# Latent attention with both parts of the exponentials taken from PSUM, and the softmax sums taken beside the values

## The chip, the core and the metric

The kernel runs on one core of a Trainium2 chip. The metric is the device time of one execution in microseconds (us); lower is better. Five engines work side by side, each through its own instructions in order: PE (TensorE, matrix products into PSUM), DVE (VectorE), ACT (ScalarE), POOL (GpSimd) and SP, which here issues the transfers.

## What is computed

The reference is a backbone of two layers. The change lies in one mixer of the first layer, the latent attention: 8 heads, queries and keys of 96 numbers, values of 64. There are 1024 sample tokens, which read 256 cached context tokens and the 1024 sample tokens, and 256 prompt tokens, which read only themselves.

```python
def mla_keys_values(ckv, kpe, w_kv_b, k_norm):
    kv = (ckv @ w_kv_b).reshape(b, s, H_A, NOPE_DIM + V_DIM)
    k_nope, v = kv[..., :NOPE_DIM], kv[..., NOPE_DIM:]
    ...
def one_block(qblk):
    s = jnp.einsum('bqhd,bkhd->bhqk', qblk, k, preferred_element_type=jnp.float32) * scale
    p = jax.nn.softmax(s, axis=-1).astype(v.dtype)
    return jnp.einsum('bhqk,bkhd->bqhd', p, v)
...
att = block_attention(q, k, v).reshape(b, s, W_A) * jax.nn.silu(g_a)
```

All of it is float32. The kernel gets float32 accuracy from products of a rounded type (fp32r) by splitting each operand into a rounded high part and the small rest, and adding the products high*high, high*low and low*high.

## The kernel before

The attention (`mla`) is written as a list of 176 **steps** (the code calls them slots). A head has three **groups** of queries: G1 (tokens 0 to 511) and G2 (512 to 1023), each against 10 chunks of 128 keys, and G3 (the 256 prompt tokens) against 2 chunks. A step is one chunk of keys for one group, so a head has 10 + 10 + 2 = 22 steps. The order of the instructions on PE, ACT, DVE and POOL is the order in which the program is written (`chained`), and each engine takes its instructions strictly in that order. Within a step the order is set by the table `MORD`; work that belongs to a group but not to a chunk is hung on a step by `at(step, function)`.

What a step does:

- `mla_score`: three products on PE give the transposed scores of one chunk in a PSUM tile `x` (128 keys x 512 queries). Minus the maximum of a query is already in them, as row 96 of the operands.
- ACT takes the exponential of `x` to `p` (SBUF, L1415) and copies it to the rounded part `ph` (L1416).
- `mla_lo`, one step later: DVE subtracts `pl = p - ph` (L1426; POOL for chunk 4), and POOL adds `p` to the running sum `pacc` (L1431).
- `mla_av`, five steps later (`LAG`): two products add `ph` and `pl` against the 128 columns [value high | value low] of the chunk to the PSUM tile `av` (L1439).
- `mla_max` and, a step later, `mla_min`: a tile of 128 queries of a coming group gets its scores in leading parts, in one PSUM tile `S` of three banks (L1364), and DVE takes the maximum over its 1280 columns (L1392). There is one such tile, so the next `mla_max` waits for the `mla_min` before it. `MAHEAD` says how many steps ahead of its group each stands. `mla_shift` then puts the maxima into the queries (four PE transposes, one ACT copy, two steps ahead of the group).

What ends a group: `mla_sums` (the sums of `pacc` over the keys by products with one column of ones), `mla_inv` (DVE's reciprocals of 4 numbers per partition), `mla_row` (four transposes spread them over the rows), `mla_copy` (ACT copies one half of `av`, L1462), `mla_out` (DVE adds the other half, L1467, one step after the copy) and `mla_gate` (ACT copies the inverses; for odd heads POOL multiplies with the gate and the values, L1478 and L1482). `MEND` holds the steps on which these stand.

The PSUM banks of this stage: 3 for `S`, 2 for `x`, 1 for the transposes `pt`, 2 for `av`. The values come from `prep_k`, which writes them split to DRAM (`d_V`), and `load_head` reads a head's back. Behind the last step, `out0_steps` (the output projection) fills waiting PE with products listed in `FILL`; its last row of operands needs the gated result of the last two heads (`out0_mix(3, ...)`).

Of the kernel before, what the change touches and what calls it, by code (L numbers as in the profile page):

```python
# [18 lines left out]
P = 128  # L19
# [6 lines left out]
EPS = 1e-6  # L26
# [12 lines left out]
ACCV = 7  # L39
FILL = (0, 0, 1, 0, 0, 0, 1, 1, 1, 1, 1, 1, 1, 0, 0, 0, 0)  # L40
# [10 lines left out]
PLO = (4,)  # L51
PB = LAG + 2
MORD = ('load_head', 'out0_mix_load', 'out0_mix', 'out0_w', 'mla_av', 'mla_inv', 'mla_min', 'mla_lo', 'mla_max', 'mla_copy', 'mla_out', 'mla_shift', 'mla_gate', 'mla_row', 'load_k', 'mla_sums')
# [13 lines left out]
class Rows:  # L67
    """Exact float32r parts of [1024, tokens], a tile for each group of tokens: [:, k, tokens of one group]."""
# [17 lines left out]
class Kern:  # L86
# [17 lines left out]
    def chained(self, *engines):  # L104
        """What is traced inside issues in the order of the trace on each of engines."""
# [18 lines left out]
    def rsqrt_steps(self, pool, out, ss, n, width):  # L124
        """out = (ss / n + EPS) ** -0.5, by the integer seed and three Newton steps."""
# [16 lines left out]
    def split_w(self, src, n, short=False, tag="w"):  # L142
        """DRAM [128, n] -> exact float32r parts in SBUF; short: in less time, with a half on DVE."""
# [60 lines left out]
    def main(self, ctx):  # L204
# [5 lines left out]
        # scratch in DRAM  # L210
# [69 lines left out]
    def mod_rows(self, ps, rows, tag, bufs=None):  # L280
        """2 * silu of both conditions, on every partition; yields before each of the four copies."""
# [138 lines left out]
    def start_square(self, scr, o, y, eng):  # L420
        """Sums over half y of d, but for the partitions, of the squares of 256 tokens."""
# [5 lines left out]
    def start_sum(self, scr, sums, y):  # L427
        """Sums over the partitions; of two tiles of tokens at columns 2 * y + tile."""
# [12 lines left out]
    def start_h(self, t, hh, hl, r, o, n, k):  # L441
        """Block k of h of tokens o..o+n; r: rows of rstd."""
# [63 lines left out]
    def mod_gate(self, lp, pr):  # L506
        """Two blocks of the gate of layer 1, with the same rows; the last of them ends it."""
# [26 lines left out]
    def small_start(self, sp, wp):  # L534
# [3 lines left out]
        # gains of the transposed rows  # L538
# [45 lines left out]
    def small_out(self, sp):  # L584
# [45 lines left out]
        # rotary key, gain in; the sum of squares of the raw key tail  # L630
# [13 lines left out]
        # rotary tables with the query gain in  # L644
# [60 lines left out]
    def mlstm_stab(self):  # L705
        """The stabilisers from chunk to chunk, and the weights of the states with them; yields between its small steps."""
# [19 lines left out]
    def gate_silu2(self, out, ps):  # L726
        """out = 2 * silu(ps)"""
# [4 lines left out]
    def gate_unit(self, pool, hh, hl, u, dst, groups=GROUPS, bufs=2):  # L732
        """2 * silu of a block of columns, to DRAM; yields between its groups of tokens."""
# [40 lines left out]
    def stream(self, units, hh, hl):  # L774
        """Projections by blocks of 128 columns; yields between their products. The last unit's weights are only made ready."""
# [17 lines left out]
    def drive(self, main, side):  # L793
        """The products of main, and between them the steps of side, which yields how many columns may pass before its next."""
# [6 lines left out]
    def mlstm(self, mp, hh, hl, hs):  # L801
        """The heads' projections, and between their products the steps of the heads' other work."""
# [109 lines left out]
        # decay matrices  # L912
# [32 lines left out]
        # states at the start of each chunk  # L945
# [26 lines left out]
        # outputs  # L972
# [164 lines left out]
    def prep_k(self, pp, s, x):  # L1137
# [12 lines left out]
        V = pp.tile([P, 4, P], F32R, name="V", tag="V", bufs=3)  # L1150
        pv = ps.rearrange("p (s h e) -> p s h e", s=2, h=4)
        nc.scalar.activation(tok[:, :, 0:64], pv[:, 0], AF.Copy)
        sq = pp.tile([P, 4, 64], F32, name="sqa", tag="sqa", bufs=2)
        nc.scalar.activation(sq, pv[:, 0], AF.Square)
        nc.scalar.activation(V[:, :, 0:64], pv[:, 1], AF.Copy)
        nc.vector.tensor_tensor(V[:, :, 64:P], pv[:, 1], f(V[:, :, 0:64]), op=ALU.subtract)
        nc.sync.dma_start(self.d_V[4 * hf:4 * hf + 4, :, i, :].rearrange("h p e -> p h e"), f(V))
# [57 lines left out]
    def prep_head(self, pool, s, h):  # L1215
        """Scaled transpose of a head's [tok, 96] tiles as float32r parts, to DRAM."""
# [20 lines left out]
    def mla(self):  # L1237
        """Transposed scores of a head's group of queries against a chunk of 128 keys per step; the maximum of a query
        is taken ahead, over the scores of the leading parts, and enters the product as a row of its operands."""
# [4 lines left out]
        with ExitStack() as es:  # L1244
            self.ps_x = es.enter_context(self.pool(name="psAx", bufs=2, space=PSUM))
            self.ps_t = es.enter_context(self.pool(name="psAt", bufs=1, space=PSUM))
            self.ps_s = es.enter_context(self.pool(name="psAs", bufs=2, space=PSUM))
# [3 lines left out]
            groups, slots, jobs, todo = [], [], {}, {}  # L1251

            def at(s, fn, *a):
                todo.setdefault(s, []).append((fn, a))
            for h in range(8):
                for o, n in GROUPS:
# [11 lines left out]
                    e, w = len(slots) - 1 + LAG, MEND[n]  # L1268
                    at(e + w[0], self.mla_copy, heads, G)
# [1067 lines left out]
```

## Time and profile before

| what | value |
|---|---|
| three timed runs | 1816.31, 1817.76 (median), 1823.14 us |
| profiled execution, span from first to last instruction | 1810.9 us |
| median minus this span | 6.9 us |
| busy shares over the span | PE 94%, DVE 70%, ACT 48%, POOL 46% |
| attention, from the first score product to the last | 625.4 to 953.1 us, 327.7 us, 41.0 us a head |

The profile has no time of its own for the profiled execution beside its span; the 6.9 us are what lies around it and what runs differ by. The busy shares are means over stages with different limits, so the stage of the attention has to be read by itself: which engine is busy there, and which wait ends last.

### The profile page before, as it was taken

How to read it: one execution, taken by the hardware profiler on the slowest of the kernel's cores; microseconds unless marked ns; L12 is line 12 of the kernel's file. 1: busy time of each engine (PE TensorE's matmuls, PEld its weight loads, DVE VectorE, ACT ScalarE, POOL GpSimd, SP SyncE). 2: the span in 40 equal slices, each digit the busy share in tenths (PEclk: the TensorE clock that was granted, in tenths of full speed). 3: DMA queues.
4: the chain of work that ended last, by engine and by line, in shares of the span. 5: the costliest groups of instructions: out<-in, count | busy, mean ns of one | idle time of the engine just before them, and what ended most of it. 6: DMA issues, size and time to landing. Idle time of an engine off the chain costs nothing.

```text
span 1810.9 us, 27853 instructions
## 1 busy us (share of the span) xinstructions
PE 1701.9 (94%) x9238; PEld 1468.2 (81%) x9238; DVE 1259.9 (70%) x3221; ACT 870.1 (48%) x1976; POOL 840.5 (46%) x783
## 2 busy tenths in 40 slices
PE   7799899999999989998899999999999999899999
PEld 7688788887878777776778879999888888788877
DVE  6878985788884899999994386556551221788852
ACT  4455665454534477777773343322111111678740
POOL 3534551113131288878884552335232321577741
PEclk9899999999999999989899999999999999999999
DMA  7326675233421372323205442447681112888836
GB/s 250 107 77 184 203 216 187 58 117 56 114 73 31 106 193 78 89 78 89 75 24 175 158 159 94 163 160 272 215 217 67 64 45 81 244 233 231 241 126 192
DMA packets 145601, 250.97 MB, mean 139 GB/s; under 512 B 21554, under 2 KB 77106, under 8 KB 145458
## 3 DMA queue, kind: packets, MB, share of 16 engines
q1 hardware_dynamic: 145314, 248.54, 45.9%
q8 instruction: 73, 1.20, 0.3%
q14 instruction: 70, 0.57, 0.1%
q0 software_dynamic: 144, 0.66, 0.1%
HBM read 167.71 MB, written 81.43 MB: 138 GB/s over the span
## 4 chain that ended last, share of the span: by engine, by line
PE 61%; DVE 23%; DMA 5%; issue 5%; ACT 3%; SPq 1%; POOL 1%; DVEq 0%; ACTq 0%; POOLq 0%
PE mm L842 9%; PE mm L170 5%; PE mm L169 5%; PE mm L168 5%; DVE pl L1426 4%; PE mm L1752 3%; PE mm L1750 3%; PE mm L1751 3%; DVE st L1392 2%; PE mm L785 2%; PE av L2184 2%; PE av L1439 2%; PE mm L1913 1%; PE mm L1592 1%; PE mm L1593 1%
## 5 line engine op out<-in xcount | busy, mean ns | idle before, releaser
L151 POOL TENSOR_TENSOR wl<-ws,wh 128x1024 fp32r<-128x1024 f32 (+1 forms) x60 | 148.6, 2478 | 354.9 <-ACT wh L149 323.3
L1426 DVE TENSOR_TENSOR pl<-p,ph 128x512 fp32r<-128x512 f32 (+1 forms) x161 | 208.3, 1326 | 4.9 <-ACT ph L1416 4.5
L1431 POOL TENSOR_TENSOR pacc<-pacc,p 128x512 f32<-128x512 f32 x125 | 188.9, 1511 | 19.3 <-ACT p L1415 12.6
L170 PE MATMUL mm<-h1h,wl 128*128 128x512 f32 (+1 forms) x480 | 171.6, 357 | 0.0
L168 PE MATMUL mm<-h1h,wh 128*128 128x512 f32 (+1 forms) x480 | 171.5, 357 | 0.0
L169 PE MATMUL mm<-h1l,wh 128*128 128x512 f32 (+1 forms) x480 | 171.5, 357 | 0.0
L842 PE MATMUL mm<-hl,wh 128*128 128x512 f32 (+1 forms) x432 | 164.7, 381 | 0.0
L842 PE MATMUL mm<-hh,wh 128*128 128x512 f32 (+1 forms) x432 | 162.9, 377 | 0.0
L842 PE MATMUL mm<-hh,wl 128*128 128x512 f32 (+1 forms) x432 | 161.6, 374 | 0.0
L1415 ACT ACTIVATE p<-x 128x512 f32<-128x512 f32 (+1 forms) x176 | 101.1, 575 | 78.9 <-PE x L1411 53.6
L149 ACT ACTIVATE wh<-ws 128x1024 fp32r<-128x1024 f32 x60 | 63.4, 1057 | 115.4 <-PE mm L169 61.6
L1416 ACT ACTIVATE ph<-p 128x512 fp32r<-128x512 f32 (+1 forms) x176 | 107.8, 612 | 5.6
L1750 PE MATMUL mm<-awh,h1h 128*128 128x384 f32 x320 | 108.6, 339 | 0.0
L1752 PE MATMUL mm<-awh,h1l 128*128 128x384 f32 x320 | 107.5, 336 | 0.0
L1751 PE MATMUL mm<-awl,h1h 128*128 128x384 f32 x320 | 107.4, 336 | 0.0
L169 PEld LDWEIGHTS mm<-h1l,wh 128*128 128x128 f32 x480 | 90.2, 188 | 14.7
L170 PEld LDWEIGHTS mm<-h1h,wl 128*128 128x128 f32 x480 | 90.3, 188 | 14.4
L168 PEld LDWEIGHTS mm<-h1h,wh 128*128 128x128 f32 x480 | 90.2, 188 | 14.5
L1392 DVE TENSOR_REDUCE st<-S 128x1 f32<-128x1280 f32 (+1 forms) x68 | 94.0, 1382 | 5.5 <-PE S L1364 5.3
L842 PEld LDWEIGHTS mm<-hh,wl 128*128 128x128 f32 x432 | 82.7, 191 | 8.5
L842 PEld LDWEIGHTS mm<-hh,wh 128*128 128x128 f32 x432 | 82.7, 192 | 8.5
L842 PEld LDWEIGHTS mm<-hl,wh 128*128 128x128 f32 x432 | 82.7, 192 | 7.9
(474 smaller groups left out, 5075.1 us busy)
## 6 DMA issues: line engine op xcount, KB each, us to landing
adar<-adaR SPq DMA_DIRECT2D x64, 256.0 KB, 2.8
ws<-evB SPq DMA_DIRECT2D x24, 512.0 KB, 3.7
ws<-odB SPq DMA_DIRECT2D x20, 512.0 KB, 3.4
d_V<-V SPq DMA_DIRECT2D x32, 256.0 KB, 2.5
ws<-wout SPq DMA_DIRECT2D x16, 512.0 KB, 3.4
k<-d_k SPq DMA_DIRECT2D x7, 1152.0 KB, 11.0
q<-d_q SPq DMA_DIRECT2D x7, 960.0 KB, 6.7
Vh<-d_V SPq DMA_DIRECT2D x8, 768.0 KB, 5.0
```

The source lines that it names most:

```text
L151: nc.gpsimd.tensor_tensor(lo[:, :m], st[:, :m], f(hi[:, :m]), op=ALU.subtract)
L168: nc.tensor.matmul(ps[:, :n], a, hh[:, k, o:o + n], start=(k == 0), stop=False)
L169: nc.tensor.matmul(ps[:, :n], a, hl[:, k, o:o + n], start=False, stop=False)
L170: nc.tensor.matmul(ps[:, :n], b, hh[:, k, o:o + n], start=False, stop=(k == KB - 1))
L842: nc.tensor.matmul(ps[:, :n], (wh, wh, wl)[z % 3][:, k * P:(k + 1) * P], (hh, hl, hh)[z % 3][:, k, o:o + n], start=(z == 0), stop=(z == 3 ...
L1392: self.nc.vector.tensor_reduce(out, src, axis=AX.X, op=ALU.max, negate=True)
L1416: nc.scalar.activation(hi[:, :n], p[:, :n], AF.Copy)
L1426: eng.tensor_tensor(lo[:, :n], p[:, :n], f(hi[:, :n]), op=ALU.subtract)
L1431: eng.tensor_tensor(G["acc"][:, :n], (G["acc"] if kc > 1 else G["p"][0][0])[:, :n], p[:, :n], op=ALU.add)
L1750: nc.tensor.matmul(ps[:, :N], a, wh[:, k, :], start=(k == 0), stop=False)
L1751: nc.tensor.matmul(ps[:, :N], a, wl[:, k, :], start=False, stop=False)
L1752: nc.tensor.matmul(ps[:, :N], b, wh[:, k, :], start=False, stop=(k == KB - 1))
```

## The change

Six parts, all in the attention and in the layout of its values:

1. ACT takes the exponential twice from the PSUM tile `x`: once to the rounded `ph` in SBUF, once back into `x` itself. `p` is gone. DVE's `pl` is `x - ph`, with `x` in PSUM. `x` therefore stays in use until `mla_lo` has read it. There are three `x` tiles now, and `mla_shift` takes its transposes from the same three.
2. `pacc` on POOL adds up `ph`. The values carry a block of 64 columns of ones ([low | high | ones] for even heads, [ones | high | low] for odd). `ph` is multiplied with [low | high] into `av0`, `pl` with [high | ones] into `av1`, so the sums of `pl` grow beside the values in `av1`.
3. `mla_sums` is one plain float32 product of a block [zeros | ones] with `pacc` over all the queries, into `av1`. The four small products, the small reciprocals and the four transposes are gone.
4. Chunk 9 (the last chunk of G1 and G2) has no parts: one exponential, no subtraction, no place in `pacc`, and one plain float32 product of [high | ones] with `p` into `av1`; its values are kept whole in the place of the high part.
5. `mla_out`: ACT copies halves of `av0` and `av1`, DVE adds twice, all on one step. For odd heads `mla_gate` has DVE take a reciprocal of 128x512 (128x256 for G3). `av0` and `av1` have one tile each, so a group's first value product waits for the `mla_out` before it; the value products start three steps (`AVGAP`) behind the end of the group before, and go two chunks a step until they have caught up.
6. `MORD` puts `mla_sums` and `mla_out` ahead of `mla_lo`, and `mla_lo` ahead of `mla_min`; POOL no longer takes any subtraction; `load_V` reads values into two lasting tiles, in pieces of 512 bytes.

```diff
-MEND = {512: (1, 2, 0, 1, 1, 2, 3), 256: (1, 2, 0, 4, 1, 2, 5)}
+NAT = 9
-PB = LAG + 2
-MORD = ('load_head', ..., 'mla_av', 'mla_inv', 'mla_min', 'mla_lo', 'mla_max', 'mla_copy', 'mla_out', 'mla_shift', 'mla_gate', 'mla_row', 'load_k', 'mla_sums')
+AVGAP = 3
+PB = LAG + 4
+MORD = ('load_head', ..., 'mla_av', 'mla_sums', 'mla_out', 'mla_lo', 'mla_min', 'mla_max', 'mla_shift', 'mla_gate', 'load_k', 'load_V')
 ...
-            self.ps_x = es.enter_context(self.pool(name="psAx", bufs=2, space=PSUM))
-            self.ps_t = es.enter_context(self.pool(name="psAt", bufs=1, space=PSUM))
-            self.ps_s = es.enter_context(self.pool(name="psAs", bufs=2, space=PSUM))
+            self.ps_x = es.enter_context(self.pool(name="psAx", bufs=3, space=PSUM))
+            self.ps_v = es.enter_context(self.pool(name="psAv", bufs=1, space=PSUM))
 ...
+                    e = end + AVGAP
+                    for c in range(G["nk"]):
+                        e = max(e, G["first"] + c + LAG)
+                        avs.setdefault(e, []).append((G, c))
+                        if len(avs[e]) == 2:
+                            e += 1
+                    end = max(x for x in avs)
+                    at(end, self.mla_sums, G)
+                    at(end + 1, self.mla_out, heads, G)
+                    at(end + 2, self.mla_gate, heads, G)
 ...
     def mla_score(self, hp, heads, G, kc):
-        nc.scalar.activation(p[:, :n], S[:, :n], AF.Exp)
-        nc.scalar.activation(hi[:, :n], p[:, :n], AF.Copy)
+        if kc == NAT:
+            nc.scalar.activation(p[:, :n], S[:, :n], AF.Exp)
+            return
+        nc.scalar.activation(hi[:, :n], S[:, :n], AF.Exp)
+        nc.scalar.activation(S[:, :n], S[:, :n], AF.Exp)
     def mla_lo(self, hp, G, kc):
-        eng = nc.gpsimd if kc in PLO and not end else nc.vector
-        eng.tensor_tensor(lo[:, :n], p[:, :n], f(hi[:, :n]), op=ALU.subtract)
+        nc.vector.tensor_tensor(lo[:, :n], S[:, :n], f(hi[:, :n]), op=ALU.subtract)
 ...
+        if kc == NAT:
+            nc.tensor.matmul(av[1][:, :n], f(one), p[0][:, :n], start=False, stop=False)
+            return
+        nc.tensor.matmul(av[0][:, :n], both, p[0][:, :n], start=(kc == 0), stop=last)
+        nc.tensor.matmul(av[1][:, :n], one, p[1][:, :n], start=(kc == 0), stop=False)
+    def mla_sums(self, G):
+        self.nc.tensor.matmul(G["av"][1][:, :n], self.zo[:, c:c + P], G["acc"][:, :n], start=False, stop=True)
+    def mla_out(self, heads, G):
+        nc.scalar.activation(v, a[other, :n], AF.Copy)
+        nc.scalar.activation(r, b[other, :n], AF.Copy)
+        nc.vector.tensor_tensor(v, a[mine, :n], v, op=ALU.add)
+        nc.vector.tensor_tensor(v, b[mine, :n], v, op=ALU.add)
     def mla_gate(self, heads, G):
+        nc.vector.reciprocal(r, r)
```

How the instructions stand now, at the end of G2 of head 0. On DVE, `pl` rows are `mla_lo`, `st` rows with 1280 columns read are `mla_min`, `pv` rows are `mla_out`. Before:

```order
L1392 TENSOR_REDUCE st<-S 128x1
L1426 TENSOR_TENSOR pl<-p,ph 128x512
L1451 RECIPROCAL st<-pt 128x4
L1426 TENSOR_TENSOR pl<-p,ph 128x512
L1467 TENSOR_TENSOR pv_7400<-av,pv_7400 64x512
```

The same place on DVE in the changed kernel:

```order
L1452 TENSOR_TENSOR pl<-x,ph 128x512
L1488 TENSOR_TENSOR pv_7400<-av_7675,pv_7400 64x512
L1489 TENSOR_TENSOR pv_7400<-av_7676,pv_7400 64x512
L1452 TENSOR_TENSOR pl<-x,ph 128x512
L1414 TENSOR_REDUCE st<-S 128x1
L1452 TENSOR_TENSOR pl<-x,ph 128x512 x2
```

There are two additions now, and they stand ahead of the step's `mla_lo` and `mla_min`; before, the one addition stood behind `mla_lo`, a step after the copy that it needs.

ACT at the same place, changed kernel, where `pv` and `pr` are the two copies that the additions and the gate need:

```order
L1441 ACTIVATE ph<-x 128x512
L1442 ACTIVATE x<-x 128x512
L1486 ACTIVATE pv_7400<-av_7675 64x512
L1487 ACTIVATE pr_7403<-av_7676 64x512
```

Both copies stand behind both exponentials of their own step; before, one copy stood there, and the copy to `pr` three exponentials later.

PE at the same place, changed kernel: the end of G2 (chunk 9, then the sums), a maximum, the scores of the next two steps, and the next maximum:

```order
L1467 MATMUL av_7676<-p,Vh_7339 128x512
L1476 MATMUL av_7676<-pacc,zo 128x512
L1386 MATMUL S<-k_7337,q 128x512 x2
L1386 MATMUL S<-k_7337,q 128x256
L1431 MATMUL x<-q,k_7337 128x512
L1432 MATMUL x<-q,k_7337 128x512
L1433 MATMUL x<-q,k_7337 128x512
```

Behind these come the three score products of one more step and then the next three `S` products, with no value products between. In the kernel before, PE stands thus there, with value products in every step:

```order
L1439 MATMUL av<-pl,Vh 128x512
L1364 MATMUL S<-k_7337,q 128x512 x2
L1364 MATMUL S<-k_7337,q 128x256
L1409 MATMUL x<-q,k_7337 128x512
L1410 MATMUL x<-q,k_7337 128x512
L1411 MATMUL x<-q,k_7337 128x512
L1439 MATMUL av<-ph,Vh 128x256
L1439 MATMUL av<-pl,Vh 128x256
```

So the two steps behind a group's end have moved from five products each to the three score products, and the steps after them carry seven.

More of the change, by code (lines that the diff above doesn't have):

```diff
@@ L50 @@
 LAG = 5
-PLO = (4,)
-PB = LAG + 2
-MORD = ('load_head', 'out0_mix_load', 'out0_mix', 'out0_w', 'mla_av', 'mla_inv', 'mla_min', 'mla_lo', 'mla_max', 'mla_copy', 'mla_out', 'mla_shift', 'mla_gate', 'mla_row', 'load_k', 'mla_sums')
+AVGAP = 3
+PB = LAG + 4
+MORD = ('load_head', 'out0_mix_load', 'out0_mix', 'out0_w', 'mla_av', 'mla_sums', 'mla_out', 'mla_lo', 'mla_min', 'mla_max', 'mla_shift', 'mla_gate', 'load_k', 'load_V')
 DB = 128
@@ L1250, in mla @@
             self.load_pair(hp, heads, 0)
-            groups, slots, jobs, todo = [], [], {}, {}
+            self.zo = hp.tile([P, 192], F32, name="zo")
+            nc.gpsimd.memset(self.zo, 1.0)
+            nc.gpsimd.memset(self.zo[:, 64:P], 0.0)
+            groups, slots, avs, todo = [], [], {}, {}
             def at(s, fn, *a):
                 todo.setdefault(s, []).append((fn, a))
+            end = -AVGAP
             for h in range(8):
@@ L1285, in mla @@
             with self.chained(E.PE, E.Activation, E.DVE, E.Pool):
-                groups[0]["st"] = hp.tile([P, 8], F32, name="st", tag="st", bufs=5)
-                for s in range(min(todo), max(max(todo), len(slots) + LAG) + 1):
+                for s in range(min(todo), max(todo) + 1):
                     if 0 <= s < len(slots):
@@ L1292, in mla @@
                             self.mla_lo(hp, *slots[s - 1])
-                        if m == "mla_av" and 0 <= s - LAG < len(slots):
-                            self.mla_av(heads, *slots[s - LAG])
+                        if m == "mla_av":
+                            for x in avs.get(s, []):
+                                self.mla_av(heads, *x)
                         for fn, a in todo.get(s, []):
@@ L1301, in mla @@
                         fill = self.out0_steps(A, 0, self.pre, 0, KB - 1)
-                    if s >= len(slots) + FILL[0]:
-                        for _ in range(FILL[1 + s - len(slots) - FILL[0]]):
-                            next(fill, None)
+                    if s >= len(slots) and FILL[s - len(slots):][:1] == (1,):
+                        next(fill, None)
+                for _ in fill:
+                    pass
             self.out0_mix(3, 0, 512, src=heads[7][4][:, 0:512])
@@ L1327, in load_head @@
             self.kts += [self.mlap.tile([P, 2, 1536], F32R, name=f"k{x}") for x in range(3)]
+            self.vts = [self.mlap.tile([P, 12, 192], F32R, name=f"Vh{x}") for x in range(2)]
+            for x, c in enumerate((P, 0)):
+                nc.gpsimd.memset(f(self.vts[x][:, :, c:c + 64]), 1.0)
         k = self.kts[h % 3]
-        V = self.mlap.tile([P, 12, P], F32R, name="Vh", tag="Vh", bufs=2)
+        V = self.vts[h % 2]
         if h > 0:
@@ L1422, in mla_lo @@
         n = G["n"]
-        p, hi, lo = G["p"][kc]
-        end = (G["h"], G["o"]) >= (7, 512)
-        eng = nc.gpsimd if kc in PLO and not end else nc.vector
-        eng.tensor_tensor(lo[:, :n], p[:, :n], f(hi[:, :n]), op=ALU.subtract)
+        if kc == NAT:
+            return
+        hi, lo, S = G["p"][kc]
+        nc.vector.tensor_tensor(lo[:, :n], S[:, :n], f(hi[:, :n]), op=ALU.subtract)
         if kc == 1:
-            G["acc"] = hp.tile([P, 512], F32, name="pacc", tag="pacc", bufs=3)
+            G["acc"] = hp.tile([P, 512], F32, name="pacc", tag="pacc", bufs=2)
@@ L1429, in mla_lo @@
         if kc > 0:
-            eng = nc.vector if end and (kc >= ACCV or G["o"] == TS) else nc.gpsimd
-            eng.tensor_tensor(G["acc"][:, :n], (G["acc"] if kc > 1 else G["p"][0][0])[:, :n], p[:, :n], op=ALU.add)
+            nc.gpsimd.tensor_tensor(G["acc"][:, :n], G["acc"][:, :n] if kc > 1 else f(G["p"][0][0][:, :n]), f(hi[:, :n]), op=ALU.add)
     def mla_av(self, heads, G, kc):
         nc = self.nc
-        n, V = G["n"], heads[G["h"]][2]
+        n, V, y = G["n"], heads[G["h"]][2], G["h"] % 2
@@ L1436, in mla_av @@
         if kc == 0:
-            G["av"] = self.ps_s.tile([P, 512], F32, name="av", tag="av")
-        for x in (1, 2):
-            nc.tensor.matmul(G["av"][:, :n], V[:, G["kb"] + kc, :], G["p"][kc][x][:, :n], start=(kc == 0 and x == 1),
-                             stop=(kc == G["nk"] - 1 and x == 2))
-    def mla_sums(self, hp, G):
-        nc = self.nc
-        nt = G["n"] // P
-        G["r"] = pt = self.ps_t.tile([P, 512], F32, name="pt", tag="t") if nt == 4 else G["av"][:, 256:512]
-        for x in range(nt):
-            nc.tensor.matmul(pt[:, x:x + 1], G["acc"][:, x * P:(x + 1) * P], self.ones[:, 0:1], start=True, stop=True)
@@ L1449, in mla_inv @@
-    def mla_inv(self, G):
-        nt = G["n"] // P
-        self.nc.vector.reciprocal(G["st"][:, 4:4 + nt], G["r"][:, 0:nt])
-    def mla_row(self, G):
-        for x in range(G["n"] // P):
-            self.nc.tensor.transpose(G["r"][:, x * P:(x + 1) * P], G["st"][:, 4 + x:5 + x].to_broadcast([P, P]), self.ident)
-    def mla_copy(self, heads, G):
+            G["av"] = [self.ps_v.tile([P, 512], F32, name=f"av{x}", tag=f"av{x}") for x in range(2)]
+        av, p, c = G["av"], G["p"][kc], G["kb"] + kc
@@ new lines, in mla_av @@
+        both, one = V[:, c, 64 * y:64 * y + P], V[:, c, 64 - 64 * y:192 - 64 * y]
+        if kc == NAT:
+            nc.tensor.matmul(av[1][:, :n], f(one), p[0][:, :n], start=False, stop=False)
+            return
+        last = kc == (G["nk"] if G["nk"] <= NAT else NAT) - 1
+        nc.tensor.matmul(av[0][:, :n], both, p[0][:, :n], start=(kc == 0), stop=last)
+        nc.tensor.matmul(av[1][:, :n], one, p[1][:, :n], start=(kc == 0), stop=False)
+    def mla_sums(self, G):
+        n, c = G["n"], 64 - 64 * (G["h"] % 2)
+        self.nc.tensor.matmul(G["av"][1][:, :n], self.zo[:, c:c + P], G["acc"][:, :n], start=False, stop=True)
```

58 lines of the change are left out of this document (29 added, 29 removed).

## The prediction

> **What bounds the kernel now.** I read the busy time of the attention's stage first, then its groups by shape, then its waits, then the instructions one by one. The header of the first row is PE, PEld (weight loads), DVE, ACT, POOL, granted PE clock, DMA share, GB/s.
>
> ```profile
> span 1810.9 us, 27853 instructions
> 625.90:958.00 332.10, 296.80 (x1373) 235.40 (x1371) 320.22 (x284) 243.69 (x429) 272.91 (x186) 0.94 0.33 91
> L1409 PE MATMUL x<-q,k x176: 283/399/775, 625.4 to 953.1; 97*128 97x512 f32 x160, 97*128 97x256 f32 x16
> ...
> L1426 DVE TENSOR_TENSOR pl<-p,ph 128x512 fp32r<-128x512 f32 x145 | 193.7, 1363 | 4.8 <-ACT ph L1416 4.5
> L1416 ACT ACTIVATE ph<-p 128x512 fp32r<-128x512 f32 x160 | 101.1, 632 | 5.1
> L1415 ACT ACTIVATE p<-x 128x512 f32<-128x512 f32 x160 | 95.1, 595 | 78.7 <-PE x L1411 53.6 <-issue 14.8 <-POOL pacc L1431 6.6
> L1467 DVE TENSOR_TENSOR pv<-av,pv 64x512 f32<-64x512 f32 x16 | 10.9, 684 | 0.2
> L1462 ACT ACTIVATE pv<-av 64x512 f32<-64x512 f32 x16 | 9.5, 591 | 3.1 <-PE av L1439 2.8
> L1517 ACT ACTIVATE mxh<-mxl,sc 128x512 fp32r<-128x512 f32 x7 | 4.9, 707 | 0.0
> ...
> PEld S L1364 <- DVE st L1392: 30.0, 19, 3.1
> PE S L1364 <- DVE st L1392: 22.1, 17, 2.7
> ```
>
> DVE is busy 320.2 of 332.1 us: it is the bound. Its subtractions take 193.7 of that. PE (296.8, and its records overlap) waits for DVE's maxima. The 176 scores run from 625.4 to 953.1: 327.7 us, 41.0 a head of 22 steps.
>
> The subtraction is slow for a reason that single rows show:
>
> ```profile
> 947.23 1.77 DVE L1426 TENSOR_TENSOR pl<-p,ph 128x512 fp32r<-128x512 f32 x1
> 715.54 0.65 DVE L1426 TENSOR_TENSOR pl<-p,ph 128x512 fp32r<-128x512 f32 x1
> 652.86 1.41 DVE st L1392
> 706.23 0.40 PE L1411 MATMUL x<-q,k 96*128 96x512 f32 x1
> 706.46 0.40 PE L1439 MATMUL av<-ph,Vh 128*128 128x512 f32 x1
> ...
> 706.94 0.75 PE L1364 MATMUL S<-k,q 96*128 96x512 f32 x3
> 707.53 0.40 PE L1409 MATMUL x<-q,k 97*128 97x512 f32 x1
> ...
> 519.79 0.38 PE L1040 MATMUL cps<-kT,qT 128*128 128x128 f32 x2
> 520.01 0.60 PE L1041 MATMUL cps<-Cst,qT 128*128 128x258 f32 x2
> ```
>
> The same subtraction takes 0.65 or 1.77 us; the addition with one operand in PSUM (L1467) averages 0.684, like the short one. PE starts a 512-column product every 0.23 us (706.23 to 706.46) and needs 0.59 for the three of a maximum (706.94 to 707.53). A plain float32 product comes as two records: 0.22 us for 128 columns (519.79 to 520.01), so four times that, 0.87, for 512.
>
> **The change, part by part.** *Subtraction.* 18 a head at 0.68 (L1467's row) in place of 1.363; ends 0.65 and 1.36 (if POOL still holds it up). I take 0.68, since one operand is in PSUM as in that row. DVE's work per head is then 18 x 0.68 + 8 maxima x 1.41 + 4 additions x 0.68 + about 3 for the small shapes and the mix = 29.3 us without reciprocals, where 320.2 / 8 = 40.0 stood. *ACT.* The copy of 0.632 becomes an exponential that ends in PSUM. No row writes there from ACT; the nearest is 0.595 (L1415), which I take. Below, 0.5 would change each gap under 0.1 us; above, if reading and writing one bank excluded each other, 1.19. *Chunk 9.* PE 0.87 for two products (0.46), minus one subtraction. *Sums.* 0.87 for eight small records and four transposes of about 1.2: even. So PE's work per head is 20 x 3 + 18 x 2 products x 0.233 + 8 x 0.59 + 5 plain ones, 4 of 0.87 and one of half, + 3.4 for G3's shapes and the shifts = about 33.4 us. *Values.* The parts in `prep_k` have as many elements as before. Loads of 512-byte pieces are wanted some 16 steps after they are issued, and the longest load of before took 14.0 us; `load_V` waits on SP for a head's last products, and behind it queue loads of the coming head. Nothing, with 30 us of cover. The memsets on POOL lie ahead of the first step.
>
> So by work alone PE would be the bound and 8 x (41.0 - 33.4) would be won. But PE, ACT and DVE take their instructions in order, and an `x` tile is now free only after `mla_lo`. I followed the order through one head with these durations; PE stands still in three places (steps counted from a head's first chunk).
>
> *End of G2 (step 2).* From the end of the sums product: maximum 0.59, score 0.70 and 0.16 to its last column, two exponentials 1.19, copy `pv` 0.59, two additions 1.37, `mla_lo` 0.68, `mla_min` 1.41, and about 0.15 of handing over: 6.85 us, and only then may the next `mla_max`, on step 4, write `S`. PE has the maximum and two scores meanwhile, 2.0 us. It idles 4.9. The additions are the turn: they wait for ACT's copies, which stand behind the exponentials of their own step, and `mla_lo` and `mla_min` wait behind them on DVE, ready long since.
> *End of G3 (step 5).* The same on step 6 with half-size pieces: score 8 needs the tile of score 5, whose `mla_lo` stands behind the additions. PE idles 2.1, and 0.4 for the maximum that the shift needs.
> *End of G1 (step 14).* From the last column of score 15: exponentials 1.24, mix copy 0.71, DVE's part of the mix and the additions 0.8 + 1.37, `mla_lo` 0.68 = 4.8; only then score 17. PE has 1.15 of it: idle 3.65.
> With 0.4 at the last shift, a head takes 33.4 + 4.9 + 2.5 + 3.65 + 0.4 = 44.8 us.
>
> *Reciprocals.* Three for each odd head, of 512, 512 and 256 per partition. The only rows are small:
>
> ```profile
> L1451 DVE RECIPROCAL st<-pt x16: 167/169/183, 656.0 to 959.5; 128x4 f32<-128x4 f32 x16
> L1451 DVE RECIPROCAL st<-av x8: 155/157/171, 682.8 to 962.9; 128x2 f32<-128x2 f32 x8
> ```
>
> Two more elements cost 12 ns, 6 ns each: 512 take 0.15 + 3.07 = 3.2 us, 256 take 1.7. The cheap end is an ordinary DVE operation, 0.68. I take 3.2, the only reciprocal rows there are. They hold up `mla_lo` and `mla_min` behind them. Followed through: G2's and G3's, on steps 4 and 7 of the next head, cost 2.9 together (their rest falls into time in which PE waits anyway), G1's on step 16 costs 2.8: 5.7 a pair of heads. At 0.68 it would be 1.1.
> The Trainium skill, "VectorE: DVE Perf Modes", section "First, the fixed hardware budget", says that the reciprocal runs an iterative divide with a repeat count of 8. If that is eight cycles an element, 512 take an estimated 4.4 us; a pair would pay 8.7 and the sum below would end at 1892.
>
> *The clock.* After idle time PE runs at half rate here (the seventh column is the granted clock; starts 0.43 apart, not 0.23):
>
> ```profile
> 653.00:656.00 3.00, 1.68 (x12) 1.60 (x13) 2.78 (x3) 1.07 (x2) 2.92 (x3) 0.98 0.22 85
> 656.00:659.00 3.00, 3.00 (x8) 2.35 (x9) 2.96 (x5) 1.23 (x2) 2.86 (x3) 0.50 0.00 0
> 657.19 0.63 PE L1439 MATMUL av<-ph,Vh 128*128 128x512 f32 x1
> 657.62 0.63 PE L1439 MATMUL av<-pl,Vh 128*128 128x512 f32 x1
> 773.00:776.00 3.00, 1.30 (x7) 0.72 (x5) 3.00 (x3) 2.91 (x6) 2.91 (x3) 1.00 0.00 0
> 776.00:779.00 3.00, 3.00 (x18) 2.65 (x19) 3.00 (x2) 0.87 (x2) 2.50 (x2) 1.00 0.00 0
> ```
>
> It happened after 1.3 us of idling at 654 and not after 1.7 at 774. Half rate for 3 us costs PE 1.6. If it follows both long gaps of every head, a pair pays 3.3 (part falls into the waiting); I count half, 1.6.
> The Trainium skill, "TensorE: Matmul & The Clock Gate", section "HAM oscillation — how this bites in real kernels", has the clock halved once idle time crosses a window of about 3.4 us. Both gaps are longer; by that rule the sum ends 7 us later, at 1886.
>
> *The end.* The last row of the output projection needs the last gate:
>
> ```profile
> 956.51 0.40 PE L1591 MATMUL S<-mxh,wh 128*128 128x512 f32 x1
> ...
> 965.72 0.39 PE L1593 MATMUL S<-mxh,wl 128*128 128x512 f32 x1
> 963.82 0.72 ACT L1517 ACTIVATE mxh<-mixa,sc 128x512 fp32r<-128x512 f32 x1 [2.77 <-POOL mixa L1482]
> ```
>
> From the last sums of G2 it is copies 1.2, additions 1.4, reciprocal 3.2, POOL's two products 2.6, split 1.5 = 9.9 us; PE has about 5.5 (seven rows of 0.70 as filling, G3's products). That is 4 us more than now, where PE hardly waits.
>
> **The sum.** A pair: 2 x 44.8 + 5.7 + 1.6 = 96.9. Four pairs 387.6, minus 2.9 that the first head doesn't inherit: 384.7. Against 327.7: +57.0, and 4 at the end: +61. The span goes from 1810.9 to 1872; with the 6.9 by which the median lies above that span, 1879 us.
>
> **The rivals.**
> 1. *The relief wins (faster).* If the engines run far enough ahead that the additions hold up nobody, odd heads are bound by DVE (29.3 + 2 x 3.2 + 1.7 = 37.4) and even ones by PE (33.4): 4 x 70.8 = 283, -41 with the end: 1777. For it speaks that DVE is the bound now by 320 of 332. Against it: the chain at step 2 is all in the written order, and one `S` tile cannot be run ahead of. It decides where PE idles under 7.6 us a head; I count 11.4.
> 2. *Cheap reciprocals.* At 0.68: 4 x (89.6 + 1.1 + 1.6) = 369, +41 and 2 at the end, 1861. Still slower; this is inside the first case.
> 3. *Slow exponential into PSUM.* At 1.19 ACT has some 41 us a head and each chain grows by 0.6: 2 to 4 more a head, 1895 to 1911. A subtraction that POOL still holds up (1.36) adds 18 x 0.68 = 12 to DVE, which at 41.5 and reciprocals goes the same way or beyond: the change would then not do what it says.
> 4. *They balance*, with gaps of 7 to 8 us a head: within 9 us of before.
>
> **How the numbers follow.** 0.66 for the forecast with its own range of 1845 to 1895 (cheap reciprocals and no halved clock at one end, slow ones and both halvings at the other); 0.14 for the third; 0.14 for the first; 0.06 for the balance. A measurement here tells changes of about 0.5% (9 us) from none: faster 0.14, same 0.06, slower 0.80. The range of 1835 to 1925 takes in the forecast and most of the third case and leaves out the first and the balance.
>
> **What would show it.** In the changed profile `pl` should take about 0.68, DVE should fall clearly below nine tenths in the stage, and the longest waits should be PE's `S` products for `st` and PE's scores for `pl`, with `pv` additions ahead of both waiting for ACT; the reciprocals should show 3 to 4 us. I am wrong if PE is busy without gaps through steps 2 to 4 and 15 to 17, if the scores span under 330 us, or if the stage is as slow as I say but for another engine.

## The result, and the profile after

The changed kernel takes 1882.6 us (median of four runs, 1879.0 to 1885.9); the kernel before, run beside it, took 1817.0. The ratio is 1.036, with a 95% interval of 1.033 to 1.039: slower by some 65 us. The forecast was 1879. The profiled execution has a span of 1880.5 us, 69.6 more than before. Each profile shows one execution, and executions of one kernel lie up to 12 us apart (the kernel before: 1811.3 to 1823.1 us), so a few us between two profiles need not come from an edit.

The first fence is the page's span line, then the row of the stage (its window, its length, then busy time of PE, PEld, DVE, ACT and POOL, granted clock, DMA share, GB/s), then the row of the 176 scores with their first and last start:

```profile
span 1880.5 us, 27299 instructions
628.00:1024.00 396.00, 319.13 (x1191) 240.29 (x1192) 247.95 (x291) 214.87 (x412) 198.00 (x162) 0.86 0.29 77
L1431 PE MATMUL x<-q,k x176: 282/396/988, 628.4 to 1022.1; 97*128 97x512 f32 x160, 97*128 97x256 f32 x16
```

DVE, which was busy 96% of this stage, is busy 63% now, so the relief that the change aims at is real. But the scores span 393.7 us where they spanned 327.7, no engine is busy all the time, and the granted clock is 0.86 where it was 0.94. The 69.6 us come apart from these rows alone: the scores start 3.0 us later (628.4 against 625.4), span 66.0 more, and what follows the last score takes 0.6 more (858.4 against 857.8).

The groups of the same stage (busy, mean ns of one, idle before them and for whom), then, from the view of the waits, PE's and DVE's longest (us in total, times, longest):

```profile
L1452 DVE TENSOR_TENSOR pl<-x,ph 128x512 fp32r<-128x512 f32 x144 | 95.0, 679 | 59.8 <-ACT x L1442 59.4
L1414 DVE TENSOR_REDUCE st<-S 128x1 f32<-128x1280 f32 x60 | 88.7, 1479 | 1.3 <-PE S L1386 1.3
L1441 ACT ACTIVATE ph<-x 128x512 fp32r<-128x512 f32 x144 | 86.0, 597 | 145.8 <-PE x L1433 142.9
L1442 ACT ACTIVATE x<-x 128x512 f32<-128x512 f32 x144 | 85.4, 593 | 0.0
L1499 DVE RECIPROCAL pr<-pr 128x512 f32<-128x512 f32 x7 | 23.4, 3342 | 0.0
L1499 DVE RECIPROCAL pr<-pr 128x256 f32<-128x256 f32 x3 | 5.2, 1741 | 0.0
...
PE x L1431 <- DVE pl L1452: 38.9, 15, 4.3
PE S L1386 <- DVE st L1414: 34.6, 8, 4.8
DVE pv L1488 <- ACT pv L1486: 31.4, 10, 4.4
```

Each operation has the price that was taken for it: the subtraction 0.679 us (0.68), the exponential into PSUM 0.593 (0.595), the reciprocals 3.34 and 1.74 (3.2 and 1.7). And the engines wait in a circle: PE for DVE's subtractions and maxima, DVE for ACT's copies, ACT (142.9 us) for PE's scores.

The circle is seen one instruction at a time at the end of G2 of head 1. The timeline gives start, duration, instruction, and in brackets the idle time of its engine before it and who ended it:

```profile
724.66 0.40 PE L1433 MATMUL x<-q,k 96*128 96x512 f32 x1
724.94 0.59 ACT L1442 ACTIVATE x<-x 128x512 f32<-128x512 f32 x1
725.55 0.59 ACT L1486 ACTIVATE pv<-av 64x512 f32<-64x512 f32 x1
726.17 0.69 DVE L1488 TENSOR_TENSOR pv<-av,pv 64x512 f32<-64x512 f32 x1 [3.81 <-ACT pv L1486]
727.00 0.69 DVE L1489 TENSOR_TENSOR pv<-av,pv 64x512 f32<-64x512 f32 x1
727.71 0.69 DVE L1452 TENSOR_TENSOR pl<-x,ph 128x512 fp32r<-128x512 f32 x1
728.31 1.48 DVE L1414 TENSOR_REDUCE st<-S 128x1 f32<-128x1280 f32 x1
729.85 1.44 PE L1386 MATMUL S<-k,q 96*128 96x512 f32 x3 [4.79 <-DVE st L1414]
730.31 3.34 DVE L1499 RECIPROCAL pr<-pr 128x512 f32<-128x512 f32 x1
731.51 0.63 PE L1432 MATMUL x<-q,k 96*128 96x512 f32 x1
```

DVE does nothing for 3.81 us and waits at the head of its queue for the copy. Behind that come `pl`, whose exponential (L1442) ended at 725.53, and the maximum, whose products ended at 723.65, one after the other, and only then may PE write `S` again: 4.79 us of idling, where 4.9 had been worked out. Behind the stop PE's products take 0.63 us, not 0.40, and start 0.43 apart, not 0.23: half rate.

### The profile page after: what moved, and what is told of

Same layout as the page of the kernel before. It is cut to its first block, busy times and chain, and to the rows that moved or that the text cites. A ratio compares the mean times of both kernels' runs of the same rounds, so it can differ in the third digit from the quotient of the medians.

```text
span 1880.5 us, 27299 instructions
## 1 busy us (share of the span) xinstructions
PE 1726.0 (92%) x9046; PEld 1473.0 (78%) x9046; DVE 1193.4 (63%) x3228; ACT 842.3 (45%) x1960; POOL 766.1 (41%) x760
## 4 chain that ended last, share of the span: by engine, by line
PE 67%; DVE 19%; DMA 4%; ACT 4%; issue 3%; POOL 1%; SPq 1%; DVEq 0%; ACTq 0%; POOLq 0%
PE mm L841 9%; PE mm L169 5%; PE mm L168 5%; PE mm L167 5%; PE mm L1773 2%; PE mm L1774 2%; PE mm L1772 2%; PE mm L784 2%; PE x L1431 2%; PE av L1471 2%; PE av L1470 2%; PE x L1433 2%; PE x L1432 2%; PE av L2206 2%; PE S L1386 2%
## 5 line engine op out<-in xcount | busy, mean ns | idle before, releaser
L1456 POOL TENSOR_TENSOR pacc<-pacc,ph 128x512 f32<-128x512 f32 x112 | 143.3, 1280 | 63.8 <-ACT ph L1441 59.4
L1441 ACT ACTIVATE ph<-x 128x512 fp32r<-128x512 f32 (+1 forms) x160 | 92.2, 576 | 148.5 <-PE x L1433 145.4
L1452 DVE TENSOR_TENSOR pl<-x,ph 128x512 fp32r<-128x512 f32 (+1 forms) x160 | 101.8, 653 | 72.1 <-ACT x L1442 71.5
L1431 PE MATMUL x<-q,k 97*128 97x512 f32 (+1 forms) x176 | 85.9, 488 | 42.2 <-DVE pl L1452 38.9
L1442 ACT ACTIVATE x<-x 128x512 f32<-128x512 f32 (+1 forms) x160 | 91.4, 571 | 0.0
```

The costliest lines, as they stand in the source:

```text
L1431: nc.tensor.matmul(S[:, :n], k[0:97, 0, c], q[0:97, 0, qs], start=True, stop=False)
L1452: nc.vector.tensor_tensor(lo[:, :n], S[:, :n], f(hi[:, :n]), op=ALU.subtract)
L1456: nc.gpsimd.tensor_tensor(G["acc"][:, :n], G["acc"][:, :n] if kc > 1 else f(G["p"][0][0][:, :n]), f(hi[:, :n]), op=ALU.add)
```

## The experiments

Each kernel was timed beside the kernel before. Differences between kernels are differences of their medians; the ratio to the kernel before has its interval. Three of the first four put right one suspect each in the changed kernel, and one (e3) moves half of the suspected order.

**The written order (e1).** The table of the order within a step:

```diff
-'mla_av', 'mla_sums', 'mla_out', 'mla_lo', 'mla_min', 'mla_max', 'mla_shift', 'mla_gate',
+'mla_av', 'mla_sums', 'mla_lo', 'mla_min', 'mla_max', 'mla_out', 'mla_shift', 'mla_gate',
```

> One edit: on a step, the subtractions, the maximum of a tile and the next tile's products stand ahead of the group's copies and additions (the table of the order within a step). Theory of the written order: the long stops come from additions that wait for late copies while ready DVE work stands behind them. Then the subtraction and the maximum behind a group's end come some 2 to 3 us sooner, a head costs about 40 us instead of 44.7, and the time falls by 25 to 60 us, most likely 45, to about 1837. The waits of the S products for st and of the scores for pl shrink to less than half. Rival 1, the reciprocals alone make the stops: they stay where they are, so under 10 us of change. Rival 2, the ring of three x tiles is too short as such, whatever the order: under 10 us of change.

Measured: 1832.3 us, ratio 1.009 (1.007 to 1.012), 50 less than the change. No work is added or taken away, and on DVE the edit only puts a subtraction and a maximum ahead of two additions, so three quarters of the loss were their order. Both rivals fall. The waits for `pl` and for `S` fell from 38.9 and 34.6 us to about half, a little short of the "less than half" that was expected. Stops were only one part of what came back: PE's idle time in the stage falls from 77 us to 50, but its busy time falls as much, from 319 us to 292, and the granted clock is 0.94 again, as in the kernel before (PE's waits in the stage, then e1's stage):

```profile
PE x L1431 <- DVE pl L1452: 20.3, 11, 2.6
PE S L1386 <- DVE st L1414: 18.9, 16, 4.2
...
628.00:970.00 342.00, 291.95 (x1174) 213.50 (x1173) 246.76 (x287) 212.13 (x408) 193.08 (x158) 0.94 0.33 88
```

**The reciprocals (e2).** The kernel leaves out the division by the softmax sums.

```diff
-        nc.vector.reciprocal(r, r)
+        nc.vector.tensor_scalar(r, r, 1.0, None, op0=ALU.mult)
```

> One edit: the reciprocal of each odd head's gate becomes an ordinary DVE operation of the same shape (a multiplication by one), so the division by the softmax sums is left out. Prediction's price: 5.7 us a pair of heads at 3.2 us a piece and 1.1 at 0.68, so four pairs should fall by about 18 us, and the end by 2: about 1862. Rival 1, the reciprocals are the main cost: 40 us or more, to 1840 or below. Rival 2, they lie beside PE's idle time: under 6 us.

Measured: 1867.3 us, ratio 1.029 (1.026 to 1.032), 15 less than the change where 18 in the stage and 2 at the end had been priced. The scores span 381.8 us here, 12 less. The reciprocals are a smaller part, as forecast; the main loss stays without them. PE's idle time stays too: in the window from 628 to 1011 it is busy 305.9 us and idle 77, as idle as with the reciprocals; what falls is its busy time, by 13 us.

**Half of the order (e3).** Only `mla_min` goes ahead of `mla_out`, `mla_lo` stays behind it.

> One edit: on a step only the maximum of a tile goes ahead of the group's additions, the subtraction stays behind them. Theory of the written order: the stop for S at the end of G2 (4.9 us predicted) nearly goes, but the scores two steps on then wait for the subtraction that is still late, and so G1's end is unchanged: 10 to 25 us less, about 1865. Rival, the stop is a matter of the single S tile alone: all of the loss at G2's end goes, 35 us or more. Rival, the reciprocals make the stops: under 6 us.

Measured: 1860.6 us, ratio 1.025 (1.022 to 1.028), 22 less, inside the first theory's range. PE's wait moves from the maximum to the subtraction behind it: PE had waited 38.9 us for `pl` and 34.6 for the maximum, and here it is 52.2 and 5.2. So the two instructions are two doors in a row, and one open door gives less than half of what both give.

```profile
PE x L1431 <- DVE pl L1452: 52.2, 21, 4.3
PE S L1386 <- DVE st L1414: 5.2, 12, 1.7
```

**Chunk 9 (e4).** `NAT = 99` instead of 9, so that no chunk is a plain product.

> One edit: chunk 9 is treated like the others (two exponentials, a subtraction, a place in the sum, two products of the rounded type). Prediction's prices: two plain products less and four of 0.233 us more a head are 0.8 us less on PE, and two subtractions of 0.68 and two exponentials of 0.59 a head more on DVE and ACT, but at a group's end every step of the chain waits for ACT, so from -8 to +12 us, most likely +4. Rival, the plain float32 products cost PE more than their records show and PE's work is what counts: 10 us or more less.

Measured: 1872.2 us, ratio 1.032 (1.029 to 1.036), 10 less than the change, outside the range of -8 to +12. My +4 was wrong, and the rival's sign and size were right, but not its reason, that the products cost more than their records show. The timeline of the change shows the plain product at the price that had been taken (two records, 721.20 to 722.06, 0.86 us):

```profile
721.20 1.02 PE L1467 MATMUL av<-p,Vh 128*128 128x512 f32 x2
722.06 1.02 PE L1476 MATMUL av<-pacc,zo 128*128 128x512 f32 x2
```

PE starts a rounded product every 0.23, so two of those take 0.46: chunk 9 as a plain product costs PE 0.40 more, twice a head, 6.4 us in all. That was counted, and then ACT and DVE were expected to eat it up, which they did not. The other 3 to 4 us are not accounted for.

**Order and chunk 9 together (f1).**

> Two edits together, each run alone before: subtraction and maximum ahead of the copies and additions (1832), and chunk 9 treated like the others (10 us less than the change). If the two are separate costs (PE's written order, PE's plain products), they add: about 1822, between 1815 and 1828. Rival: what the plain products cost was waiting that the new order has removed as well, so nothing more comes: 1830 to 1836.

Measured: 1833.1 us, ratio 1.008 (1.005 to 1.012): nothing beyond e1, so the two do not add, and the rival's number holds. What takes up the 10 us with the new order this run does not show. DVE, with its two more subtractions a head, is the suspect; f2 and g2 bear on it.

**The reciprocal in slices (f2).** The longest stop left in e1 (timeline, DVE and PE):

```profile
715.41 3.34 DVE L1499 RECIPROCAL pr<-pr 128x512 f32<-128x512 f32 x1
718.67 0.63 DVE L1452 TENSOR_TENSOR pl<-x,ph 128x512 fp32r<-128x512 f32 x1
719.22 1.48 DVE L1414 TENSOR_REDUCE st<-S 128x1 f32<-128x1280 f32 x1
720.75 1.43 PE L1386 MATMUL S<-k,q 96*128 96x512 f32 x3 [4.17 <-DVE st L1414]
```

The reciprocal stands ahead of a ready subtraction and a ready maximum, just as the additions had stood. f2 puts it behind f1 in four pieces, one a step:

```diff
-                    at(end + 2, self.mla_gate, heads, G)
+                    for x in range(n // P if h % 2 else 0):
+                        at(end + 2 + (x if h < 7 else 0), self.mla_rec, G, x)
+                    at(end + (1 + n // P if h % 2 and h < 7 else 2), self.mla_gate, heads, G)
 ...
```

> As the last one, and the reciprocal of a gate is cut into slices of 128 columns, one a step, so that no more than about 0.95 us of it (0.15 and 128 times 6.25 ns) stands ahead of the next step's subtraction and maximum; the work is the same, 0.5 us a gate more. Theory: with the new order the one long stop left at the end of G2 of odd heads (4.17 us) is the reciprocal ahead of them: 8 to 20 us less than the last one, about 1809. Rival: DVE's work counts and not where it stands: no change or up to 4 us more.

Measured: 1832.2 us, ratio 1.007 (1.005 to 1.010): no change against f1. A miss for the theory; the rival, that DVE's work counts and not where it stands, has the number. A slice took 0.934 us as expected, and the 4.17 us stop fell to 1.77, but the 342 us of the stage show new small ones behind it: the time went from one stop to several. f1 had these two rows of PE's waits at 19.1 us and 2.7 (there L1386 and L1389); with another 2.8 us, in which the transposes of `mla_shift` wait for the same maxima, they come to 21.5 here:

```profile
PE S L1388 <- DVE st L1416: 12.1, 18, 1.8
PE S L1391 <- DVE st L1416: 6.6, 7, 2.1
```

**The mix and the memset (f3).**

```diff
-'out0_mix_load', 'out0_mix', 'out0_w', ..., 'mla_max', 'mla_out',
+'out0_mix_load', 'out0_w', ..., 'mla_max', 'out0_mix', 'mla_out',
 ...
+            nc.gpsimd.memset(f(self.kts[0][96:97, 0, :]), 1.0)
             self.vts = [self.mlap.tile([P, 12, 192], F32R, name=f"Vh{x}") for x in range(2)]
 ...
-        nc.gpsimd.memset(f(self.kts[0][96:97, 0, :]), 1.0)
```

> As the last one, and two moves: the split of the mix of the output projection (ACT 0.70, DVE 0.81) behind the subtraction and the maximum of its step, and the row of ones of the keys ahead of the ones of the values on POOL. Theory: 1.4 us at each of seven stops at G1's end, and the first score some 1 to 3 us sooner: 8 to 13 us less than the last one, about 1799, so clearly faster than the kernel before. Rival: the stop at G1's end stays because the copies of the mix on ACT still delay the next exponentials: 1 to 4 us less.

Measured: 1822.9 us, ratio 1.003 (1.001 to 1.006), 9 less than f2, as the theory had it; but the 1799 that was expected had counted on f2's gain too, and the kernel is not faster than the one before. The run does not separate the two moves; g3 bears on the second. PE's waits for `pl` went from 15.6 to 2.3 us, and a good part came back one step later, as a wait of the value products for the additions, which now stand behind the mix:

```profile
PE av L1472 <- DVE pv L1490: 11.5, 11, 2.0
```

**The memset alone, in the changed kernel (g3).**

> The changed kernel with one move: the row of ones of the keys ahead of the ones of the values on POOL. Theory: the late start (first score at 628.4 where the kernel before has 625.4) is these memsets alone, so the first score comes at 625 to 626, the time falls by 3 us and the stage behind it stays at 393.6. Rival: something else ahead of the stage is late (the split of the values): the first score stays at 628.

Measured: 1876.9 us, ratio 1.033 (1.030 to 1.036), 6 less than the change; the two intervals overlap, so how much of that is real stays open. The scores start at 624.8 instead of 628.4, a little earlier even than the theory had it, and span 392.8 instead of 393.7. But only a third of those 3.6 us is the memsets. In the changed kernel POOL writes the ones of the values ahead of the row of the keys for which the first score waits, and PE stands still 0.92 us for that. The rest arises ahead of the stage: the last instruction of POOL before the memsets (`hs`), which none of the experiments touches, starts at 618.41 in the kernel before, at 621.40 in the changed kernel and at 618.89 here. From it to the first score it is 6.97, 7.00 and 5.87 us. So the move is worth 1.1 us, and against the kernel before the memsets cost next to nothing; f1 and f2, which do not have the move, start at 625.8 and 625.0. The first row is of the kernel before, the next three of the changed kernel, the last of this run:

```profile
618.41 1.04 POOL L991 TENSOR_TENSOR hs<-hs,rsh 128x512 f32<-128x512 f32 x1 [11.59 <-DVE rsh L139]
621.40 1.04 POOL L990 TENSOR_TENSOR hs<-hs,rsh 128x512 f32<-128x512 f32 x1 [11.59 <-DVE rsh L138]
625.50 1.41 POOL L1344 MEMSET Vh<- 128x768 f32 x2 [3.07 <-PE mm L841]
626.97 1.37 POOL L1327 MEMSET k<- 1x1536 f32 x1
L1431 PE MATMUL x<-q,k x176: 282/396/988, 624.8 to 1017.6; 97*128 97x512 f32 x160, 97*128 97x256 f32 x16
```

**Other places (f4).** From f3, with the reciprocal whole again:

```diff
-MAHEAD = {0: (12, 9, 7, 4), 512: (10, 8, 6, 4), 1024: (12,)}
+MAHEAD = {0: (12, 9, 7, 4), 512: (12, 9, 7, 4), 1024: (12,)}
-MIXAT = 37
+MIXAT = 43
 ...
-LAG = 5
+LAG = 4
 ...
-                        if len(avs[e]) == 2:
+                        if len(avs[e]) == 3:
```

> From the run with the mix and the memset moved, with the reciprocal whole again, four edits to where things stand: G2's four maxima 12, 9, 7 and 4 steps ahead instead of 10, 8, 6, 4 (so that none of them falls on the two steps behind the end of a group's reciprocal), the value products four steps behind instead of five and up to three chunks a step when they catch up, and the mix six steps later. The durations of the rows, walked through the written order engine by engine, give 25 us less than for the run before it: about 1798, between 1785 and 1812, faster than the kernel before. Rival: PE's and DVE's work and the halved clock bound it by now, not the places: 1815 to 1830.

Measured: 1809.9 us, ratio 0.996 (0.995 to 0.998): 13 less than f3, inside the range but only half of the 25, and a little faster than the kernel before. Which of the four edits brought it, no run shows.

**The respaced kernel without reciprocals (g2).** The edit of e2, on f4; the kernel again leaves out the division by the sums.

> The respaced kernel with the reciprocal replaced by a DVE operation of ordinary length (the division by the softmax sums is left out). Theory: where the places are right, DVE's work of some 35 us a head is near PE's 33, and the reciprocals' extra 27 us over the stage still cost about half of themselves: 10 to 18 us less than the respaced kernel. Rival: they are covered now, under 4 us.

Measured: 1783.1 us, ratio 0.983 (0.980 to 0.985), 27 less than f4, more than the 10 to 18 that were expected. The twelve reciprocals take 8 x 3.34 + 4 x 1.74 = 33.7 us of DVE, and their stand-ins 5.6 (eight of 0.42 and four of 0.57 in e2): DVE has 28 us less to do, and the kernel is 27 faster. In the changed kernel the same edit had given 15. In f4, PE's one large wait is for the subtraction, 15.0 us in 7 stops, each behind a reciprocal of 512; in g2 that wait is gone and the clock is granted in full. Rows of f4's waits, f4's stage and g2's stage:

```profile
PE x L1431 <- DVE pl L1452: 15.0, 7, 2.8
...
628.00:944.00 316.00, 285.03 (x1165) 208.94 (x1164) 253.84 (x299) 215.10 (x418) 213.18 (x171) 0.95 0.35 92
...
628.00:921.00 293.00, 273.24 (x1168) 200.07 (x1167) 233.00 (x300) 215.37 (x420) 214.75 (x171) 0.99 0.38 100
```

**A small reciprocal (h1).** The 128 rows of `pr` hold only two different rows of sums, 64 times each. So they are taken out, inverted as 128x8, and spread again, by transfers, for three of the four pairs of heads (the gate then comes nine steps later, and the loads for the mix four, which the cut below leaves out):

```diff
+    def mla_rec(self, hp, G):
 ...
+        d = self.d_rs[0, G["id"], 0:2 * n]
+        for y in range(2):
+            nc.sync.dma_start(d[y * n:y * n + n].rearrange("(o e) -> o e", o=1), r[64 * y:64 * y + 1, :n])
+        G["t"] = t = hp.tile([P, 8], F32, name="rt", tag="rt", bufs=3)
+        nc.sync.dma_start(t[:, :n // 64], d.rearrange("(p e) -> p e", e=n // 64))
+    def mla_inv(self, G):
 ...
+        nc.vector.reciprocal(t[:, :n // 64], t[:, :n // 64])
+        d = self.d_rs[1, G["id"], 0:2 * n]
+        nc.sync.dma_start(d.rearrange("(p e) -> p e", e=n // 64), t[:, :n // 64])
+        for y in range(2):
+            nc.sync.dma_start(r[64 * y:64 * y + 64, :n], d[y * n:y * n + n].partition_broadcast(64))
```

> The respaced kernel with the reciprocals of the first three pairs of heads taken small: the two rows of 512 sums that differ go by transfers through DRAM into a tile of 128x8, DVE inverts that (four steps later), and two more transfers spread the inverses back over the 128 rows before POOL's gate (nine steps later than before); the last pair stays as it is. The run without reciprocals gave 26.7 us for four pairs. Theory: DVE's time at these places is what counts, so three quarters of it comes back, less small losses: 14 to 20 us less than the respaced kernel, about 1792, clearly faster than the kernel before. Rival: DVE or POOL now waits for the transfers (six of them in a chain through SP, behind which the loads of the next heads queue): less than 6 us, or slower.

Measured: 1787.0 us, ratio 0.983 (0.980 to 0.986): 23 less than f4, more than the 14 to 20 that were expected; 32 less than the kernel before, 96 less than the change. It is the fastest kernel of this study with the whole computation, and faster than both kernels of the comparison. Its small reciprocals, what DVE waited for them, the stage, and the PE wait that had been 15.0:

```profile
L1507 DVE RECIPROCAL rt<-rt 128x8 f32<-128x8 f32 x6 | 1.2, 198 | 3.5 <-DMA rt<-d_rs 3.5
...
628.00:925.00 297.00, 274.44 (x1170) 200.50 (x1170) 231.72 (x301) 216.35 (x422) 212.16 (x170) 0.99 0.42 107
...
PE x L1437 <- DVE pl L1458: 1.0, 2, 0.7
```

DVE waited 3.5 us in all for the transfers; the rival's stop did not come. PE is busy 92% of the stage now.

## Why the prediction was right

**The cause** was the one that was named. The walk through the order gave the places and the sizes of the stops before there was a trace of them, and e1 took three quarters of the loss away by the order alone. The first four stops behind G2 in the trace are 4.67, 4.79, 4.72 and 4.79 us (4.9 forecast); those behind G1 lie between 2.70 and 3.98 (3.65); those behind G3 are 1.54, 0.55, 1.71 and 1.60 (2.1). That the time came within 4 us is in part luck, as the terms below show.

**The rivals.** The relief did not win: DVE is at 63%, and it is not the bound. It could have: h1 and g2 show the relief once order, places and reciprocals let it through (stage about 300 us; the first rival had said 283). The reciprocals are not cheap (3.34). The exponential into PSUM is no slower than into SBUF, and the subtraction is 0.679 at its mean, so neither half of the third rival came. Whether the subtraction is faster for its operand in PSUM, as was argued, or because POOL has less to do beside it (198 us busy in the stage, 273 before), no run here separates. The balance fell with the time.

**Terms that were off.** The forecast's 1879 against 1882.6 hides misses of both signs:

| term | forecast | measured |
|---|---|---|
| stage | +57.0 | +66.0 |
| ahead of the stage | 0 | +3.0 |
| end | +4 | +0.6 |
| sum, span | +61 | +69.6 |
| median above the span | 6.9 | 2.1 |
| reciprocals in the stage | 18 more than cheap ones | 12 by e2 |

The last but one is a matter of the executions that were profiled: that of the kernel before lies 6.9 us under its median, that of the changed kernel 2.1. In the medians the change costs 65.5.

*PE's work* has a slip in its addition: the terms that are named (96 products of 0.233, 8 maxima of 0.59, 4.5 plain products of 0.87, 3.4) come to 34.4 us a head, not 33.4. Over eight heads that is 8 of the 9 us by which the stage was put too short; with it the forecast would have been 1887.

*The clock* is the term that was much too small, and the idling was put too large by about as much. 1.6 us a pair had been counted for half rate, 6 us in all. In windows of 1 us over the stage the granted clock shows 21 slow stretches: twelve of 3.4 us, eight of 6.8 and one of 13.6, together 109 us at half rate. That is a shortfall of 55 us, where the kernel before has 20. The longest stretch is that behind the stop at 729.85; behind the other stops of G2 it is 6.8 us each (columns as in the stage's row; the granted clock is the third figure from the end):

```profile
728.00:732.00 4.00, 2.15 (x6) 1.77 (x7) 4.00 (x4) 0.00 (x0) 0.00 (x0) 0.71 0.00 0
732.00:736.00 4.00, 3.91 (x12) 2.81 (x11) 3.59 (x3) 1.44 (x3) 2.14 (x2) 0.50 0.21 61
740.00:744.00 4.00, 3.49 (x12) 2.65 (x10) 4.00 (x5) 1.56 (x3) 1.64 (x3) 0.59 0.00 0
```

The shortfall is not added to the time in full. By the terms put right, PE had 275 us of work at full rate, and with 11.4 us of idling a head and the reciprocals some 111 of idle time. The trace has 319 busy and 77 idle. PE was 44 us longer at work, where 6 were counted, and 34 shorter idle. So "idle" and "half rate" were not separate terms to be added, and that the two misses nearly cancel is luck. No run here could hold the clock up and so show it alone; e1 had the stops and the slow time fall together.

The Trainium skill, "TensorE: Matmul & The Clock Gate", section "HAM oscillation — how this bites in real kernels", has the clock halved by idle gaps beyond about 3.4 us. The stops of 4.7 us agree with it. But in e1 a stop of 2.04 us was followed by half rate too (0.63 us a product, in place of 0.40), in the changed kernel one of 1.37 us (632.73), while one of 2.70 us (659.37) was not; there the measurement decides. The two rows of e1:

```profile
742.40 0.50 PE L1431 MATMUL x<-q,k 97*128 97x512 f32 x1 [2.04 <-DVE pl L1452]
743.06 0.63 PE L1433 MATMUL x<-q,k 96*128 96x512 f32 x1
```

*The start* was costed at nothing, since "The memsets on POOL lie ahead of the first step". They do, but the first score waits 0.92 us for the last of them. Even so the nothing holds against the kernel before: the +3.0 of the table were there before the memsets began, as the rows under g3 show.

*The end* was put 3.4 us too late. The chain came as described (1026.12 for the last sums of G2, 1034.68 for the split), but PE had more filling products than the 5.5 us that I took, and stood still only for 1.53:

```profile
1034.68 0.72 ACT L1539 ACTIVATE mxh<-mixa,sc 128x512 fp32r<-128x512 f32 x1 [4.67 <-POOL mixa L1504]
1035.45 0.50 PE L1613 MATMUL S<-mxh,wh 128*128 128x512 f32 x1 [1.53 <-ACT mxh L1539]
```

*The reciprocals* were priced as further idling of PE behind `mla_lo` and `mla_min`, 5.7 us a pair. That step failed: PE idles 77 us with them and 77 without (e2). Their 12 us in the stage, where 18 had been counted, came as busy time of PE, with 109 us at half rate against 92 in e2 (a shortfall of 55 against 46). They cost 15 us where they stood, and 27 once the rest was in order: a price of a thing is a price at its place.

## What to carry to other kernels

On in-order engines, look at what stands behind a waiting instruction before you count what an engine saves: two short additions that waited for late copies, written ahead of ready work, cost 50 us here and hid the relief of the busiest engine. Put consumers of late results last in their step, count what the stops do to the clock as well, and then look again, since the next instruction that stands in the way (here the mix, then the reciprocal) shows only when the first is gone. Where a slow operation works on rows that repeat, shrink it and move the data instead: 3.34 us of DVE became 0.2 and a few transfers.

## What the hardware showed that was not expected

- The reciprocal costs 3342 ns for 512 elements a partition, 934 for 128, 1741 for 256, 198 for 8: about 6.2 ns an element and some 0.14 us on top. The 6 ns an element, forecast from two rows that differ by two elements, held within 5% up to 512. The Trainium skill, "VectorE: DVE Perf Modes", section "First, the fixed hardware budget", has a repeat count of 8, from which 4.4 us had been estimated; the measured 3.34 is three quarters of that.
- An exponential that reads a PSUM tile and writes the same tile takes 593 ns, and one into SBUF 597: no price for either.
- In the stage of the changed kernel half rate came in stretches of 3.4 us, 6.8 and once 13.6, while PE was busy for nearly all of the time; it followed stops of 1.4 to 4.8 us, but not the one of 2.70.
